# Layer 0's two feed-forwards as one, value projections of 512 columns, and 32 low parts made during block 1

## The chip, the cores and the metric

The kernel runs on one core of a Trainium2 chip. The metric is the device time of one execution in microseconds (us).

## The reference

Two residual blocks over 256 tokens of 1024 features. The first block runs once; the second has two layers over a token stream `x` and a context stream `ctx`. Cut to the parts that the change touches:

```python
def _ffn(h, p):
    return (jax.nn.silu(h @ p['w_ff_gate']) * (h @ p['w_ff_up'])) @ p['w_ff_down']

for l in range(DEPTH_2):                                  # 2 layers
    hc = _modulate(xc, mod_c[0], mod_c[1])
    if last:
        mem = _context_memory(hc, p)
    else:
        yc, mem = _context_mixer(hc, p)                   # attention, GLA, convolution, gates
        xc = _post(xc, yc, mod_c[2], ln1_g[l], ln1_b[l])
        xc = _post(xc, _ffn(_modulate(xc, mod_c[3], mod_c[4]), p), mod_c[5], ln2_g[l], ln2_b[l])
    x = _post(x, _latent_mixer(_modulate(x, sh1, sc1), mem, cos, sin, p), g1, ln1_g[l], ln1_b[l])
    x = _post(x, _ffn(_modulate(x, sh2, sc2), p), g2, ln2_g[l], ln2_b[l])
```

Both streams use the same weights in layer 0, the mixer's and the feed-forward's. Everything is float32.

## The kernel before

Activations lie with features on the partitions, 8 tiles of 128 features by 256 tokens. All weights are packed into "units" of 128 x 1024 float32 (512 KB), read one after another in the order in which the program asks for them (`unit`, L438). `unit` loads the raw unit four ahead (SP's DMA queue, 5 buffers) and splits it two ahead (`load`, L455): ScalarE writes the high part `whi` as float32r, GpSimd or VectorE writes the low part `wlo` = raw - high (`split`, L420; `lo_eng`, L373, deals them out by a ratio for each phase, `LO`: 1 of 2 on GpSimd in block 1 and layer 0's feed-forward, 1 of 3 in block 1's feed-forward, 3 of 5 in layer 0's mixers). `whi` and `wlo` have 3 buffers each. A product is three float32r products (`mm3`, L472): high x high, weight high x activation low, weight low x activation high; for a unit that is 24 matmuls of 256 columns. In layer 1 some parts multiply the raw float32 unit instead (`native`).

Layer 0's mixer runs twice with the same 109 units, for the context and then for the tokens. The first run stores each low part in DRAM (`kept`), the second reads it back in place of computing it. Projections that need tokens on the partitions (values) go through `tok` (L515): the activation is the stationary operand, the weight moves, 256 columns at a time; the names are `memv`, `foxv`, `sbv`, `v0`, `vg0`. In `mix` (L1449) a fixed interleaving steps attention, the units `glu0`, the gated-linear-attention levels (`gF`, `cum`, `am`) and, at low priority, the convolution `ca` on VectorE, 31 steps a tile; then come `gb0_0`, `r0`, `gb1_0`, `gb2_0` and `out0`.

After the two mixers layer 0's feed-forward runs for the context, then for the tokens: 44 gate/up units and 24 down units each (8 of them with 6 blocks in place of 8). While one stream's units run, the other stream's layer norms (`post`, `modulate`) run on VectorE and ScalarE, and 12 steps of the next layer's modulation matmuls (`ada`) are put in between. A scheduler orders each engine's instructions by the program's order and priorities; engines run their queues in order. Matmul results use three PSUM buffers (`mmp`).

The change touches `_plan`, `_pack`, `unit`/`load`, `block1`, `mem_kv`, `fox`, `stick`, `gla_in`, `gla_pair`, `gla_state`, `modulate`, `mix` and `program`.

## Time and profile before

| | |
|---|---|
| median of 3 runs | 3046.5 us (3044.25 to 3047.64) |
| profiled execution, its own time | 3039.65 us |
| its span, first to last instruction | 3037.4 us |
| mean granted TensorE clock | 0.971 |
| TensorE matmul / weight load busy | 2808.7 us (92%) / 2638.7 us (87%) |
| VectorE / ScalarE / GpSimd busy | 1965.5 us (65%) / 1412.3 us (46%) / 919.9 us (30%) |
| DMA | 578.33 MB, mean 190 GB/s |

PE is TensorE's matmul side, PEld its weight loads, DVE VectorE, ACT ScalarE, POOL GpSimd, SP the engine whose queue issues the transfers. Busy time of matmuls is pipelined: each record is longer than the distance to the next. The granted clock is the share of full speed at which TensorE was let run. Stages, by the first unit of each: block 1's mixers to 655 us, its feed-forward to 888, layer 0's context mixer to 1376, token mixer to 1804, feed-forwards to 2245 (the context's to 2027), layer 1's memory and mixer to 2788, its feed-forward to 3017, the last norm to the end.

### The profile page before, as it was taken

The page shows a single profiled execution, that of the slowest core. Times are in us where ns is not written, and L with a number is a line of the kernel's source. Part 1 is how long each engine was busy: PE and PEld are TensorE (multiplying, and loading weights), DVE is VectorE, ACT ScalarE, POOL GpSimd, SP SyncE. Part 2 cuts the span into 40 slices and gives each one's busy share as a digit, 9 for nine tenths or more (in the row PEclk, how much of TensorE's full clock was granted, in tenths as well). Part 3 has the DMA queues.
Part 4 walks back from the last instruction along what each step waited for, and adds up shares of the span by engine and source line. Part 5 has one row for each costly group of instructions (what it writes and reads, how often), then busy time and mean ns, then how long its engine had stood idle before and what let it go on. Part 6 is the DMA issues. An engine that isn't in the chain of part 4 may idle for free.

```text
span 3037.4 us, 52212 instructions
## 1 busy us (share of the span) xinstructions
PE 2808.7 (92%) x20992; PEld 2638.7 (87%) x20992; DVE 1965.5 (65%) x3305; ACT 1412.3 (46%) x2135; POOL 919.9 (30%) x684
## 2 busy tenths in 40 slices
PE   6999999999898878799999999999999999998898
PEld 6899988888898777788899988998888787898898
DVE  7586643447855999966897354367344599674554
ACT  5465556544445433445545554445334332354443
POOL 3253322333334445540102113444320113463000
PEclk9999999999999989899999999999999999999999
DMA  5444335566466554787666887655743223354353
GB/s 191 143 156 146 126 133 174 199 238 243 149 221 236 194 202 168 256 310 281 214 245 242 326 297 259 240 188 177 247 148 116 95 97 125 112 167 139 131 177 110
DMA packets 153426, 578.33 MB, mean 190 GB/s; under 512 B 17628, under 2 KB 17756, under 8 KB 146656
## 3 DMA queue, kind: packets, MB, share of 16 engines
q1 hardware_dynamic: 152496, 574.45, 54.9%
q8 instruction: 164, 2.69, 0.4%
q10 hardware_dynamic: 688, 0.56, 0.1%
q14 instruction: 78, 0.64, 0.1%
HBM read 516.73 MB, written 58.20 MB: 189 GB/s over the span
## 4 chain that ended last, share of the span: by engine, by line
PE 45%; DVE 19%; ACT 4%; DMA 2%; POOL 1%; issue 1%; SPq 0%; ACTq 0%; DVEq 0%; POOLq 0%
PE mm L371 38%; DVE ca L364 7%; DVE gF L361 2%; PE st L371 2%; DMA raw<-in_ws 2%; PE av L371 1%; POOL wlo L361 1%; DVE wlo L361 1%; PE ga L371 1%; ACT whi L358 1%; DVE sq L361 1%; PE ad L371 1%; DVE cum L1245 1%; DVE ht L364 1%; DVE fsum L584 1%
## 5 line engine op out<-in xcount | busy, mean ns | idle before, releaser
L358 ACT ACTIVATE whi<-raw 128x1024 fp32r<-128x1024 f32 (+1 forms) x706 | 736.1, 1046 | 819.5 <-PE mm L371 527.9
L361 POOL TENSOR_TENSOR wlo<-raw,whi 128x1024 fp32r<-128x1024 f32 (+1 forms) x282 | 713.6, 2532 | 1046.5 <-ACT whi L358 827.8
L361 DVE TENSOR_TENSOR wlo<-raw,whi 128x1024 fp32r<-128x1024 f32 (+1 forms) x315 | 399.6, 1269 | 384.7 <-ACT whi L358 375.0
L371 PE MATMUL mm<-hh,whi 128*128 128x256 f32 x3376 | 506.4, 292 | 17.8 <-ACT hh L358 5.5
L371 PE MATMUL mm<-hh,wlo 128*128 128x256 f32 x3376 | 494.0, 288 | 15.2 <-DVE wlo L361 10.2
L371 PE MATMUL mm<-hl,whi 128*128 128x256 f32 x3376 | 490.8, 287 | 0.0
L371 PEld LDWEIGHTS mm<-hh,whi 128*128 128x128 f32 x3376 | 450.0, 196 | 41.5 <-ACT hh L358 8.7
L371 PEld LDWEIGHTS mm<-hh,wlo 128*128 128x128 f32 x3376 | 446.7, 195 | 18.6 <-DVE wlo L361 10.6
L371 PEld LDWEIGHTS mm<-hl,whi 128*128 128x128 f32 x3376 | 445.9, 195 | 1.5 <-issue 1.0
L364 DVE SCALAR_TENSOR_TENSOR ca<-yp,pv,ca 128x256 f32<-128x256 f32 x720 | 360.6, 555 | 2.0
L371 PE MATMUL mm<-yh,whi 128*128 128x256 f32 x1152 | 174.2, 291 | 14.3 <-ACT yh L358 11.0
L371 PE MATMUL mm<-h,raw 128*128 128x256 f32 x800 | 181.9, 381 | 0.0
L361 POOL TENSOR_TENSOR gF<-cum 128x128 f32<-128x128 f32 x192 | 99.0, 547 | 256.8 <-PE ga L371 143.9
L371 PE MATMUL mm<-yh,wlo 128*128 128x256 f32 x1152 | 168.6, 289 | 5.3 <-DVE wlo L361 4.0
L371 PEld LDWEIGHTS mm<-yh,whi 128*128 128x128 f32 x1152 | 154.4, 195 | 20.7 <-ACT yh L358 14.2
L371 PE MATMUL mm<-yl,whi 128*128 128x256 f32 x1152 | 169.4, 289 | 1.3 <-DVE yl L364 1.3
L371 PEld LDWEIGHTS mm<-h,raw 128*128 128x128 f32 x800 | 150.3, 191 | 19.3
L371 PEld LDWEIGHTS mm<-yh,wlo 128*128 128x128 f32 x1152 | 154.0, 198 | 6.5 <-DVE wlo L361 4.2
L371 PEld LDWEIGHTS mm<-yl,whi 128*128 128x128 f32 x1152 | 154.0, 197 | 2.0 <-DVE yl L364 1.6
L371 PE MATMUL mm<-hidh,whi 128*128 128x256 f32 x704 | 102.4, 286 | 0.8 <-ACT hidh L358 0.8
L371 PE MATMUL mm<-hidl,whi 128*128 128x256 f32 x704 | 101.9, 285 | 0.0
L371 PE MATMUL mm<-hidh,wlo 128*128 128x256 f32 x704 | 101.0, 284 | 0.7 <-DVE wlo L361 0.7
(283 smaller groups left out, 3808.6 us busy)
## 6 DMA issues: line engine op xcount, KB each, us to landing
raw<-in_ws SPq DMA_DIRECT2D x744, 512.0 KB, 4.0
lo<-wlo SPq DMA_DIRECT2D x109, 512.0 KB, 3.3
wlo<-lo SPq DMA_DIRECT2D x109, 512.0 KB, 4.1
wada<-in_wa SPq DMA_DIRECT2D x48, 1024.0 KB, 7.0
raw<-in_ws SPq DMA_DIRECT2D x32, 384.0 KB, 3.1
memt<-in_tok SPq DMA_DIRECT2D x4, 256.0 KB, 4.9
xt<-in_tok SPq DMA_DIRECT2D x1, 1024.0 KB, 6.2
ct<-in_tok SPq DMA_DIRECT2D x1, 1024.0 KB
```

What stands on the lines that cost most here:

```text
L358: return self.nc.scalar.activation(out, in_, f, **k)
L361: return (eng or self.nc.vector).tensor_tensor(out=out, in0=a, in1=b, op=op)
L364: return self.nc.vector.scalar_tensor_tensor(out=out, in0=a, scalar=s, in1=b, op0=op0, op1=op1)
L371: return self.nc.tensor.matmul(out, lhsT=l, rhs=r, start=start, stop=stop, **k)
L584: self.nc.vector.tensor_reduce(out=s, in_=x.rearrange("p f n -> p n f"), axis=AX.X, op=ALU.add)
L1245: nc.vector.tensor_tensor_scan(out=o, data0=self.ones_t, data1=a, initial=0.0, op0=ALU.mult, op1=ALU.add)
```

## The change

- Layer 0's feed-forward (`both_ffn`) takes both streams at once: `joint_h` keeps their high (X) and low (Y) activations side by side, and a unit's matmuls move 512 columns. The first 6 feature tiles (`LEAD`) are done for the context alone and later again for the tokens; the last down chunk is done for the context, then for the tokens. Down sums are added to the streams chunk by chunk.
- The values `memv`, `foxv`, `sbv` and `vg0` are packed for `wide`: the weight moves 512 columns, two PSUM buffers collect the two token tiles, and four units make four feature tiles of values at once.
- `ahead` reads the 32 units of `glu0` and `gb0_0` during block 1, splits them and stores the low part; both runs of the mixer then read it.
- Activations and some mixer tiles share the two places X and Y of a new pool `hj`.

```diff
     def load(self, raw, n, i, _, native):
-        if native:
+        if native is True:
             return raw, None
         hi = self.wp.tile([P, 1024], F32R, tag="whi", name="whi", bufs=3)
         lo = self.wp.tile([P, 1024], F32R, tag="wlo", name="wlo", bufs=3)
-        kept = self.kept.pop(i, None)
+        if native == "ahead":
+
+            self.split(raw, hi, lo)
+            kept = self.kept[i] = self.dp.tile([P, 1024], F32, tag=f"lo{i}", name="lo")
+            self.nc.sync.dma_start(kept, lo.bitcast(F32))
+            return None
+        kept = self.kept.get(i)
...
+    def ahead(self):
+
+        for name in ("glu0", "gb0_0"):
+            for i in range(16):
+                self.unit(POS[name] + i, native="ahead")
+                yield
...
+    def wide(self, name, c, h):
+        ps = [self.mmp.tile([P, 512], F32, tag="mm", name="mm") for _ in range(2)]
+        for u in range(4):
+            hi, lo = self.unit(POS[name] + 4 * c + u)
+            for n, (x, part) in enumerate(((h[0], hi), (h[1], hi), (h[0], lo))):
+                for t in range(2):
+                    for k in range(2):
+                        self.mm(ps[t], x[:, 2 * u + k, t * P:(t + 1) * P], part[:, k * 512:(k + 1) * 512],
+                                start=u + n + k == 0, stop=u == 3 and n == 2 and k == 1)
+            if u == 1:
+                yield
+        yield ps
...
-            weave((stick, 3), (bf, 1), (take(fill, 8), 1))
+            self.pre = self.ahead()
+            weave((stick, 3), (bf, 1), (take(fill, 8), 1), (take(self.pre, 9), 1))
             run(bf)
-            weave((self.branch(2, h, ys, acc, False), 2), (take(fill, 4), 1))
+            weave((self.branch(2, h, ys, acc, False), 2), (take(fill, 4), 1), (take(self.pre, 4), 1))
...
+    def both_ffn(self, l, xs, adas, bp):
...
+        def hidden(ft, v=None):
...
+            if v is None:
+                pg, pu = [self.mmp.tile([P, 512], F32, tag="mm", name="mm") for _ in range(2)]
+                for j, ps in enumerate((pg, pu)):
+                    self.mm3(ps, self.unit(POS[f"gu{l}"] + 2 * ft + j), both, KT, 0)
+                s, c = self.t("cv", 512), slice(0, 2 * T)
+            else:
+                pg, pu = self.proj_pair(f"gu{l}", ft, self.h_of(v))
+                s, c = self.t("cv"), slice(v * T, (v + 1) * T)
+            self.act(s, pg, AF.Silu)
+            self.tt(s, s, pu, ALU.mult)
+            self.split(s, hid[ft][0][:, c], hid[ft][1][:, c])
...
+        for ft in range(self.LEAD):
+            hidden(ft, 1)
+            yield
+        self.act(xs[0], xs[0], scale=ALPHA)
+        for ft in range(self.LEAD, CHUNKS[0]):
+            hidden(ft)
+            yield
+        for ft in range(self.LEAD):
+            hidden(ft, 0)
+            yield
...
+            if c + 1 < len(CHUNKS):
+                for f in range(KT):
+                    down(c, k, f)
+                    yield
+            else:
+                for v in (1, 0):
+                    for f in range(0, KT, 2):
+                        down(c, k, f, v)
+                        yield
...
-        step(ffn, 10)
+        for _ in range(10):
+            step(ffn, 1)
+            step(b.pre, 1)
         run(fill0)
...
+        for _ in range(4):
+            step(ffn, 1)
+            step(b.pre, 2)
+        run(ffn, b.pre)
...
+            ffn = b.both_ffn(0, (xt, ct), (ax0, ac0), bp)
+            step(ffn, 1)
+            weave((b.modulate(xt, ax0, 3, got, lambda: b.h_of(0)), 2), (take(ffn, b.LEAD - 1), 1))
+            for i in range(16):
                 step(ffn, 2)
-                for i in range(9):
-                    step(g, 2)
+                step(fill1, 1)
+            step(ffn, 10)
+            f32 = b.place("X")
+            g = chain(b.post(ct, "l2g0", "l2b0"),
+                      b.modulate(ct, ac1, 0, got, lambda: (f32[:, 0], Nones()), native=True))
+            for i in range(KT):
+                step(g, 2)
+                if i % 2:
                     step(ffn, 1)
-                run(g)
...
```

The new order on GpSimd in the context mixer, among the levels of gated linear attention (`gF`); `wlo` are low parts, `yp` edges of convolution tiles. Before:

```order
L361 TENSOR_TENSOR gF<-cum 128x128 x4
L361 TENSOR_TENSOR wlo<-raw,whi 128x1024 x2
L361 TENSOR_TENSOR gF<-cum 128x2x64 x4
L361 TENSOR_TENSOR gF<-cum 128x4x32 x4
L361 TENSOR_TENSOR wlo<-raw,whi 128x1024 x2
L361 TENSOR_TENSOR gF<-cum 128x8x16 x4
L361 TENSOR_TENSOR wlo<-raw,whi 128x1024
L361 TENSOR_TENSOR gF<-cum 128x16x8 x4
L361 TENSOR_TENSOR wlo<-raw,whi 128x1024 x2
L361 TENSOR_TENSOR gF<-cum 128x32x4 x4
L361 TENSOR_TENSOR wlo<-raw,whi 128x1024
```

and now:

```order
L366 TENSOR_TENSOR gF<-cum 128x128 x4
L366 TENSOR_TENSOR wlo<-raw,whi 128x1024
L366 TENSOR_TENSOR gF<-cum 128x2x64 x4
L366 TENSOR_TENSOR gF<-cum 128x4x32 x4
L366 TENSOR_TENSOR wlo<-raw,whi 128x1024 x2
L366 TENSOR_TENSOR gF<-cum 128x8x16 x4
L366 TENSOR_TENSOR gF<-cum 128x16x8 x4
L1509 MEMSET yp 128x15
L1510 MEMSET yp 128x15
L366 TENSOR_TENSOR gF<-cum 128x32x4 x4
```

Here 8 low parts have become 3; over the whole context mixer GpSimd has 48 in place of 67 and VectorE 13 fewer.

TensorE at the start of layer 0's feed-forward, context units (`hh`/`hl` before, `hX`/`hY` now are the activations' high and low parts); `st<-fsum` and `st<-sq` are the sums of the token stream's norms. Before, the post-norm's sum of squares is the last one in this part:

```order
L371 MATMUL mm<-hh,whi 128x256 x8
L371 MATMUL mm<-hl,whi 128x256 x7
L371 MATMUL st<-sq,ones 128x256
L371 MATMUL mm<-hl,whi 128x256
L371 MATMUL mm<-hh,wlo 128x256 x8
```

and now both sums of the modulate follow, and 24 modulation matmuls, ahead of the lead's ninth unit:

```order
L376 MATMUL mm<-hX,wlo 128x256 x8
L376 MATMUL st<-fsum,ones 128x256
L376 MATMUL mm<-hX,whi 128x256 x8
L376 MATMUL mm<-hY,whi 128x256 x8
L376 MATMUL mm<-hX,wlo 128x256 x8
L376 MATMUL mm<-hX,whi 128x256 x8
L376 MATMUL mm<-hY,whi 128x256 x8
L376 MATMUL mm<-hX,wlo 128x256 x8
L376 MATMUL st<-sq,ones 128x256
L376 MATMUL ad<-wada,sc 32x256 x24
L376 MATMUL mm<-hX,whi 128x256 x8
```

Four units later the first matmuls of 512 columns stand.

TensorE at the end of that stage (`hidh`, `hidl`: hidden features; `raw` with `h` or `hX`: layer 1's first unit). Before:

```order
L371 MATMUL mm<-hidh,whi 128x256 x6
L371 MATMUL mm<-hidl,whi 128x256 x6
L371 MATMUL mm<-hidh,wlo 128x256 x6
L1159 MATMUL ad<-cc,adas 128x128 x2
L371 MATMUL mm<-h,raw 128x256 x8
```

and now the context's modulate has its sums in the last down unit and behind it:

```order
L376 MATMUL mm<-hidh,whi 128x256 x5
L376 MATMUL st<-fsum,ones 128x256
L376 MATMUL mm<-hidh,whi 128x256
L376 MATMUL mm<-hidl,whi 128x256 x6
L376 MATMUL mm<-hidh,wlo 128x256 x6
L376 MATMUL ad<-wada,sc 32x256 x8
L376 MATMUL st<-sq,ones 128x256
L1208 MATMUL ad<-cc,adas 128x128 x2
L376 MATMUL mm<-hX,raw 128x256 x7
```

All the waits of layer 1's first unit on the context's norms, which stood among the token stream's units before, now stand in the last 8 short units and behind them.

## Rows read from the trace of the kernel before

**Rows 1.** Stages: us; busy PE, PEld, DVE, ACT, POOL; PEclk, DMA share, GB/s.
```profile
479.00:888.00 409.00, 393.74 (x3230) 362.96 (x3229) 240.56 (x311) 199.88 (x298) 131.54 (x80) 0.98 0.58 199
888.00:1376.00 488.00, 412.90 (x3018) 396.17 (x3016) 403.01 (x659) 214.61 (x312) 234.29 (x181) 0.92 0.66 231
1376.00:1804.00 428.00, 407.77 (x3091) 391.36 (x3092) 294.29 (x660) 229.16 (x332) 55.72 (x89) 0.99 0.76 272
1804.00:2245.00 441.00, 425.40 (x3584) 403.10 (x3583) 218.81 (x255) 191.20 (x277) 181.38 (x107) 0.98 0.62 216
```

**Rows 2.** TensorE timeline, first units of layer 0's feed-forward: start, us, instruction, count, idle before.
```profile
1804.37 1.12 PE L371 MATMUL mm<-hh,whi 128*128 128x256 f32 x8
1805.33 1.12 PE L371 MATMUL mm<-hl,whi 128*128 128x256 f32 x8
...
1809.35 0.70 PE L371 MATMUL st<-fsum,ones 128*128 128x256 f32 x2 [1.35 <-DVE fsum L584]
...
1818.95 0.67 PE L371 MATMUL st<-sq,ones 128*128 128x256 f32 x2 [1.97 <-DVE sq L361]
...
1831.76 2.08 PE L371 MATMUL mm<-hh,whi 128*128 128x256 f32 x8 [3.82 <-DVE cv L361]
```

**Rows 3.** TensorE timeline: one-column matmuls, then float32 of 512 and of 256 columns.
```profile
89.33 1.05 PE L371 MATMUL st<-ones,hsq 128*128 128x1 f32 x8
90.25 0.48 PE L371 MATMUL mm<-hh,whi 128*128 128x256 f32 x2
...
2276.82 7.07 PE L371 MATMUL mm<-h,raw 128*128 128x256 f32 x32
2283.72 0.81 PE L371 MATMUL mm<-raw,h 128*128 128x256 f32 x3
...
2324.20 1.02 PE L371 MATMUL st<-hsq,ones 128*128 128x512 f32 x2
2325.06 1.24 PE L371 MATMUL mm<-raw,h 128*128 128x256 f32 x5
```

**Rows 4.** Busy time from `glu0` to the end of `gb0_0`: context mixer, token mixer.
```profile
954.80:1195.70 240.90, 196.47 (x1377) 187.46 (x1376) 227.52 (x406) 100.95 (x144) 114.56 (x102) 0.90 0.55 191
1459.70:1655.40 195.70, 189.89 (x1411) 181.90 (x1410) 186.61 (x448) 98.27 (x136) 31.84 (x58) 0.98 0.65 231
```

**Rows 5.** Convolution steps, context then token mixer: ns min/median/max; then busy time of both.
```profile
L364 DVE SCALAR_TENSOR_TENSOR ca<-yp,pv,ca x225: 458/473/2673, 987.4 to 1247.5; 128x256 f32<-128x256 f32 x113
...
L364 DVE SCALAR_TENSOR_TENSOR ca<-yp,pv,ca x240: 462/482/619, 1470.0 to 1657.2; 128x256 f32<-128x256 f32 x120
...
988.00:1250.00 262.00, 145.21 (x232) 0.00 (x0) 0.89 0.55 192
```

**Rows 6.** Context mixer, instructions on `wlo` alone: us; PE, PEld, DVE, POOL busy; PEclk.
```profile
988.00:1250.00 262.00, 65.34 (x399) 57.49 (x400) 23.27 (x19) 93.46 (x31) 0.89 0.55 192
```

**Rows 7.** VectorE timeline at layer 1's start: post-norm and modulate of the token stream.
```profile
2245.18 0.87 DVE L364 SCALAR_TENSOR_TENSOR xt<-mm,ada,xt 128x256 f32<-128x256 f32 x2 [6.69 <-PE mm L371]
...
2265.30 3.65 DVE L584 TENSOR_REDUCE fsum<-xt 128x256 f32<-128x2048 f32 x1 [0.66 <-ACT xt L358]
...
2280.57 1.28 DVE L364 SCALAR_TENSOR_TENSOR ht<-xc,ada,nr 128x256 f32<-128x256 f32 x3
...
2289.05 0.46 DVE L364 SCALAR_TENSOR_TENSOR hl<-ht,ada,hh 128x256 fp32r<-128x256 f32 x1
```

**Rows 8.** The page: high parts, low parts, and the stores of low parts (KB, us to landing).
```profile
L358 ACT ACTIVATE whi<-raw 128x1024 fp32r<-128x1024 f32 (+1 forms) x706 | 736.1, 1046 | 819.5 <-PE mm L371 527.9
L361 POOL TENSOR_TENSOR wlo<-raw,whi 128x1024 fp32r<-128x1024 f32 (+1 forms) x282 | 713.6, 2532 | 1046.5 <-ACT whi L358 827.8
...
L361 DVE TENSOR_TENSOR wlo<-raw,whi 128x1024 fp32r<-128x1024 f32 (+1 forms) x315 | 399.6, 1269 | 384.7 <-ACT whi L358 375.0
...
lo<-wlo SPq DMA_DIRECT2D x109, 512.0 KB, 3.3
```

**Rows 9.** Busy time of the 20 us in which DMA moved most.
```profile
1328.00:1348.00 20.00, 17.94 (x135) 16.49 (x134) 11.77 (x11) 9.09 (x16) 9.57 (x4) 1.00 0.95 346
```

More of the change, by code (lines that the diff above doesn't have):

```diff
@@ L945, in proj_v @@
         def proj_v(f):
-            v = bp.tile([P, 2, T], F32, tag="av", name="fv", bufs=2)
-            self.act(v, self.tok("foxv", f // 2, h))
+            v = self.values("foxv", f, h, bp)
             return v
@@ L1005, in fox_turn, with values @@
         return p
+    def values(self, name, f, h, bp):
+        if f % 4 == 0:
+            self.vs = [bp.tile([P, 2, T], F32, tag="av", name="v", bufs=2) for _ in range(2)]
+            for t, ps in enumerate(self.wide_now(name, f // 4, h)):
+                for i, v in enumerate(self.vs):
+                    self.act(v[:, t], ps[:, i * T:(i + 1) * T])
+        return self.vs[f // 2 % 2]
     def softplus_abs(self, out, z):
@@ L1186, in rope, with gla_in @@
         self.tt(t, t, sw, ALU.add)
-    def gla_in(self, l, h, bp, with_q):
+    def gla_in(self, l, h, bp, with_q, room=None):
         nc = self.nc
-        qk = bp.tile([P, 4, 2, T], F32, tag="C", name="qk")
+        qk = bp.tile([P, 4, 2, T], F32, tag="C", name="qk") if room is None else \
+            room[:, 1].rearrange("p (a b) n -> p a b n", b=2)
         glr = bp.tile([P, T], F32, tag="glr", name="glr")
@@ L1210, in pair @@
                 yield
-            vg[hp] = bp.tile([P, 2, 512], F32, tag="vg", name="vg", bufs=2)
+            vg[hp] = (bp.tile([P, 4, T], F32, tag="vg", name="vg", bufs=2) if room is None else
+                      room[:, 0, 4 * hp:4 * hp + 4]).rearrange("p (a b) n -> p a b n", b=2)
+            if l == 0:
+                for got in self.wide(f"vg{l}", hp, h):
+                    for t, ps in enumerate(got or ()):
+                        self.act(vg[hp][:, t], v3(ps))
+                    yield
+                return
             for i in range(2):
-                self.act(vg[hp][:, :, i * T:(i + 1) * T], self.tok(f"vg{l}", f + i, h))
+                self.act(vg[hp][:, :, i], self.tok(f"vg{l}", f + i, h))
                 yield
@@ L1373, in modulate @@
         yield
-        h = self.new_h(pool, native)
+        h = new()
         hh, hl = h[:2]
@@ L1447, in glu, with mix @@
             yield
-    def mix(self, l, h, x, ada, mem, bp, keep, then=None):
+    def mix(self, l, h, x, ada, mem, bp, keep, then=None, room=None):
         nc = self.nc
         self.act(x, x, scale=ALPHA)
-        qk, vg, glr, gates, pairs = self.gla_in(l, h, bp, True)
+        qk, vg, glr, gates, pairs = self.gla_in(l, h, bp, True, room)
         S = mem[2] if mem else None
@@ L1484, in mix @@
         run(att, side, gla[0])
-        acc = bp.tile([P, 4, T], F32, tag="vg", name="acc", bufs=2)
+        acc = bp.tile([P, 4, T], F32, tag="vg", name="acc", bufs=2) if room is None else room[:, 0]
         acc = [acc[:, f] for f in range(4)]
@@ L1664, in program @@
+        with b.pool("m1") as bp, b.phase("m1t", t1=4, t2=6, t4=4):
+            run(b.post(xt, "l2g0", "l2b0"))
+            h = b.modulated(xt, ax1, 0, lambda: b.new_h("Y") + (f32[:, 1],), native="both")
+            b.native = True
+            mem = b.ctx_memory(1, got[3], bp, rp)
+            b.native = False
+            b.some_f32 = True
+            b.mix(1, h, xt, ax1, mem, bp, bp)
         with b.pool("f1") as bp, b.phase("f1t", t1=10, t2=6):
-            h = b.modulated(xt, ax1, 3, fast=True)
+            h = b.modulated(xt, ax1, 3, lambda: b.new_h("Y"), fast=True)
```

135 lines of the change are left out of this document (80 added, 55 removed).

## The prediction

> **What bounds the kernel now.** Read first the busy time by stage [rows 1]: each stage's own width against its engines. TensorE is near full everywhere but in one: layer 0's context mixer (888 to 1376 us) takes 488 us with a granted clock of 0.92, the token mixer behind it, which runs the same code, 428 us at 0.99. Since matmul records overlap, their busy time says little about pace, so read next the distance from start to start [rows 2]: a row of 8 float32r matmuls of 256 columns begins 0.96 us after the one ahead of it, so 0.120 us a matmul, and a weight unit (24 matmuls) costs 2.88 us.
>
> What sets the 0.120 is in [rows 3]. A plain float32 matmul instruction takes 6.90/32 = 0.216 us at 256 columns and 0.86/2 = 0.43 us at 512: twice the columns, twice the time, so this stream is set by columns, and half of 0.216 (float32 here runs each column twice as long) is 0.108. Eight matmuls of one column take 0.92, 0.115 each: what a weight load leaves as the least distance. 0.120 is nearer to the load than to the columns, so a float32r matmul of 256 columns waits for its weights.
>
> Third, the two mixers in the stretch from the first unit of `glu0` to the last of `gb0_0` [rows 4]: 240.9 us (context) and 195.7 us (tokens), VectorE busy 94% and 95%. VectorE is the bound there. The convolution step shows why its work is dearer in the first [rows 5]: median 473 ns against 482, but a longest of 2673 against 619. A step that meets one of GpSimd's low-part subtractions waits for its end. In 988 to 1250 us GpSimd makes 31 of them (93 us) and VectorE 19 (23 us) [rows 6].
>
> **Joint feed-forward, matmuls.** Removed: 48 of 136 weight units of layer 0's two feed-forwards (32 gate/up, 16 down), each with a load, a high part on ScalarE and a low part. In their place 48 units run 24 matmuls of 512 columns instead of 2 x 24 of 256: 1152 pairs of 0.240 us become matmuls of 0.43/2 = 0.215. Bounds: 0.240 (nothing gained) and 0.215; I take 0.216, from the float32 row of the same width, because the load of 0.115 is then far below the columns. 1152 x 0.024 = **-27.6 us**.
>
> The Trainium skill ("TensorE: Matmul & The Clock Gate", Back-to-back issue gap) gives 131 ns for a sustained stream of weight load and matmul at 512 columns and 216 for an isolated one. By the first the term would be 1152 x 0.109 = -126 us (an estimate); the rows have no 512-column stream under 0.215 a pass, so they speak for the second.
>
> **Joint feed-forward, its two ends.** Before, each chain (post-norm, then modulate) ran under a whole feed-forward of the other stream. Undisturbed, at layer 1's start [rows 7], the post-norm takes 2265.30 - 2245.18 = 20.1 us, the first modulated tile follows after 15.3 more, all of it 44.
>
> *Start.* The token chain now has only the lead as cover: six feature tiles of the context, 12 x 2.88 = 34.6 us. In the new order the modulate's two sums stand ahead of units 7 and 9. The first is ready at 20.1 + 3.7 (reduction) plus the low parts between, about 29 us; TensorE is there at 6 x 2.88 plus the two waits that exist already (1.35 and 1.97 [rows 2]) and half-clock matmuls, about 23: 6 idle. The second comes some 8 us later: 2.4 idle. Unit 9 then needs a PSUM buffer that VectorE frees only behind the reciprocal root, 4 more idle, as the 3.82 us wait for `cv` did before. About 15 against 7.1 now: **+8**.
>
> *End.* The context's chain starts when its last down units end; as cover stand the token stream's 8 short down units (2.16 us each, 17.3) and 8 steps of the modulation matmuls (6.9): 24 us. Layer 1's first unit needs the first modulated tile, at 35.4 us and with 5 low parts and 8 residual adds on VectorE about 42: **+16** idle (at least 35.4 - 24 = 11).
>
> *Rest.* 253 (88 gate/up units) + 127 (down) + 21 (modulation matmuls) + 3 (sums) = 404 us of matmuls stand against 441 measured [rows 1]: 37 idle, 30 without the start. With half the splits, half the weight traffic in the joint part and no second chain under a full-speed stream I take 16 of it: **-14**; bounds 0 and -25.
>
> So the stage: -27.6 + 8 + 16 - 14, about **-18 us**.
>
> **Wide values.** 40 unit runs (memory, fox and stick values 8 each, `vg0` twice 8) have 12 matmuls of 512 columns in place of 24: 480 x 0.024 = 11.5 us at most. The context mixer's 96 are under VectorE, the memory values' 96 in the waiting start; 288 x 0.024 = 6.9 count. `wide` holds two of the three PSUM buffers, about 1 us: **-6**. Moving the copies to ScalarE (the same columns, other shapes) lies beside TensorE: nothing; uncovered it is under 1 us a call.
>
> **Low parts made ahead.** In the context mixer the 32 units of `glu0` and `gb0_0` now take their low part from DRAM, as the token mixer's do in the same place without a stall that shows [rows 4]. The new order has 19 fewer low parts on GpSimd there and 13 fewer on VectorE. Direct: 13 x 1.27 = 16.5 us of VectorE [rows 8]. Indirect: the 225 convolution steps between 988 and 1250 [rows 5] would cost 225 x 0.473 = 106 at their median, and 145 less 3 for seven first steps, 142, are measured: 36 us of waiting for 31 subtractions, so 19 fewer return about 22; other instructions a few more: 42 in all. VectorE was 94% busy, so the stretch shortens by that: **-42 us**. Bounds: 16.5 (only the direct part), 60 (all of the difference between the mixers, 488 - 428).
>
> In block 1 the same 32 splits are added: 13 in the stick branch and the two gates, 10 in the last 20 gate/up units, 9 in the down projection. No matmul, but ScalarE 1.05 and GpSimd 2.53 or VectorE 1.27 each [rows 8], a 512 KB load and a 512 KB store on SP's queue. The engines have room (there VectorE is busy 241 of 409 us, ScalarE 200, GpSimd 132 [rows 1]). Two things don't: over 20 gate/up units (57.6 us) 20 loads plus 10 loads and stores are 21 MB, 364 GB/s, and the densest slice seen moved 346 [rows 9]: 3 us. And high and low parts have 3 buffers: where two ahead units follow each other (the down projection), the next real unit's split starts only when TensorE has finished the one before, about 2 us, four times: 8. Store waits on SP hold loads that are asked for four units early: nothing, else 3 us each. **+12**; bounds 0 and 32 x 3.6 = 115.
>
> **Sum.** -18 - 6 - 42 + 12 = -54 us against the profiled execution's 3039.65: 2985.7. The runs' median, 3046.5, lies 6.9 above that execution; the forecast for the median is **2992.5 us**.
>
> **The rivals.**
> 1. *VectorE's relief is only the direct part* (the mixer then waits on its attention and state chains): 25 us less gain, 3018. For it: waits for `gw`, `pr` and `am` sit in that stretch too. Against: the token mixer has them as well and needs 196 us there.
> 2. *512 columns cost 0.240*: 27.6 + 6.9 back, 3027. Against it stand the one-column and 512-column rows.
> 3. *The splits ahead are exposed*, the slower side: an ahead unit keeps one of three high/low buffers until its store has landed (3.3 us [rows 8] behind 1.05 + 2.53), and the next real unit waits. All of it exposed is 115 us, 103 above my term: 3095. From 2.0 us per ahead unit on (65 us) the change is slower than before. For it: the buffers are not increased. Against: ahead units stand mostly alone, with a real unit's 2.88 us on either side.
> 4. *A 512-column matmul keeps the distance of a 256-column one*, 0.120: 1440 x 0.096 = 138 more, 2855. The 131 ns of the Trainium skill ("TensorE: Matmul & The Clock Gate", Back-to-back issue gap) would be of this kind. Against: [rows 3] doubles.
> 5. *Both chains cost twice*: 24 more, 3017.
> 6. *Two of the gains fail together* (1 and 2): 25 + 34.5, 3052: no change.
> That the change doesn't do what it says is excluded by the order: 512-column matmuls and the missing subtractions stand in it.
>
> **How the numbers follow.** Forecast 0.64 (its own range 2965 to 3015: the mixer between 25 and 55, block 1 between 0 and 25, the ends 10 either way); rival 1 0.12, rival 2 0.08, rival 3 0.07, rival 4 0.02, rival 5 0.02, rival 6 0.05. Faster by over 0.2% (about what a measurement of this kernel can tell from no change): 0.64 + 0.12 + 0.08 + 0.02 + 0.02 = 0.88; same 0.05 (rival 6); slower 0.07 (rival 3). The range 2950 to 3032 takes in rivals 1, 2 and 5 and leaves out 3, 4, 6 (0.14) and the edges of the forecast.
>
> **What would show it.** Right: joint matmuls 0.216 apart; layer 0's feed-forward stage about 424 us with two idle groups on TensorE, near its start (waits on `fsum`, `sq`, `cv`) and before the first `hX,raw`; the stretch `glu0` to `gb0_0` of the context mixer near 199 us, with no convolution step queue behind GpSimd. Wrong: 0.240 there; that stretch over 220; block 1 (first instruction to the first unit of layer 0) longer by over 25 us.

## The result, and the profile after

| | before | after |
|---|---|---|
| median of the runs | 3045.4 us | 3006.4 us (3003.7 to 3011.5) |
| ratio, 95% interval | | 0.9884 [0.986, 0.9908] |
| profiled execution: its time, span | 3039.65, 3037.4 us | 3003.74, 3001.9 us |

The change makes the kernel 1.2% faster. The forecast was 2992.5 us with a range of 2950 to 3032: right direction, the time inside the range, the gain smaller by a quarter to a third (39 us by the medians, 35.5 by the spans, 54 said). One of the ten executions of e5_gp_dummy took 4983.3 us at a mean granted clock of 0.82; its median and range below are of the other nine. The page of the changed kernel (the part on engines, and the splitting into high and low parts):

```profile
span 3001.9 us, 48842 instructions
PE 2772.0 (92%) x19360; PEld 2536.1 (84%) x19360; DVE 1877.7 (63%) x3298; ACT 1391.0 (46%) x2095; POOL 810.6 (27%) x643
...
L363 ACT ACTIVATE whi<-raw 128x1024 fp32r<-128x1024 f32 (+1 forms) x690 | 718.4, 1046 | 819.2 <-PE mm L376 476.0
L366 POOL TENSOR_TENSOR wlo<-raw,whi 128x1024 fp32r<-128x1024 f32 (+1 forms) x232 | 579.9, 2502 | 966.7 <-ACT whi L363 654.9
L366 DVE TENSOR_TENSOR wlo<-raw,whi 128x1024 fp32r<-128x1024 f32 (+1 forms) x317 | 413.4, 1305 | 441.6 <-ACT whi L363 335.9
```

GpSimd makes 50 low parts fewer and VectorE 2 more: 48 fewer in all, one for each unit that the joint feed-forward no longer loads a second time. ScalarE makes 16 high parts fewer (48 gone, 32 made ahead). Busy time by stage in the changed kernel, columns and stages as [rows 1], by the first unit of each (start to block 1's feed-forward, that feed-forward, context mixer, token mixer, joint feed-forward, layer 1's memory and mixer), and last the stretch from `glu0` to `gb0_0` in the context mixer [rows 4]:

```profile
0.00:671.90 671.90, 614.10 (x4573) 557.13 (x4573) 392.55 (x679) 380.96 (x615) 238.35 (x134) 0.99 0.55 186
671.90:917.00 245.10, 217.98 (x1761) 206.48 (x1760) 161.71 (x203) 117.61 (x171) 72.23 (x56) 0.94 0.72 245
917.00:1357.60 440.60, 399.46 (x2914) 378.11 (x2914) 351.00 (x648) 214.69 (x313) 178.26 (x162) 0.97 0.75 263
1357.60:1784.10 426.50, 405.95 (x2999) 385.19 (x3000) 294.09 (x660) 227.83 (x330) 57.58 (x88) 0.99 0.76 272
1784.10:2211.90 427.80, 403.91 (x2427) 337.32 (x2426) 177.66 (x236) 137.53 (x191) 118.75 (x75) 0.98 0.47 164
2211.90:2786.20 574.30, 530.05 (x3075) 473.56 (x3075) 390.31 (x735) 220.21 (x348) 143.56 (x126) 0.98 0.36 119
...
988.30:1187.10 198.80, 184.77 (x1330) 173.67 (x1329) 191.23 (x428) 101.38 (x144) 65.85 (x85) 0.97 0.67 234
```

Set beside the trace of before, cut at the same units:

| stage | before, us | after, us | difference |
|---|---|---|---|
| start to the first gate/up unit of block 1 | 662.2 | 671.9 | +9.7 |
| block 1's feed-forward | 226.5 | 245.1 | +18.6 |
| layer 0, context mixer | 487.4 | 440.6 | -46.8 |
| layer 0, token mixer | 428.3 | 426.5 | -1.8 |
| layer 0, feed-forwards | 440.8 | 427.8 | -13.0 |
| layer 1 up to its feed-forward | 576.3 | 574.3 | -2.0 |
| the rest | 215.9 | 215.7 | -0.2 |

The sum is -35.5. The context mixer gave more than forecast (42), and the stretch of [rows 4] came down from 240.9 to 198.8 us (199 was said). Block 1 took back 28.3 us, and the joint feed-forward gave 13 in place of 18.

Now the joint stage from the inside. The timeline of TensorE at its start (start, us, instruction, count, idle before):

```profile
1789.06 0.70 PE L376 MATMUL st<-fsum,ones 128*128 128x256 f32 x2 [1.37 <-DVE fsum L620]
...
1798.85 0.67 PE L376 MATMUL st<-sq,ones 128*128 128x256 f32 x2 [2.13 <-DVE sq L366]
...
1813.15 1.22 PE L376 MATMUL st<-fsum,ones 128*128 128x256 f32 x2 [6.81 <-DVE fsum L620]
...
1823.12 0.67 PE L376 MATMUL st<-sq,ones 128*128 128x256 f32 x2 [1.27 <-DVE sq L366]
...
1829.02 1.21 PE L376 MATMUL mm<-hX,whi 128*128 128x256 f32 x8 [2.49 <-DVE cv L366]
...
1855.16 1.98 PE L376 MATMUL mm<-hX,wlo 128*128 128x512 f32 x8
1856.97 1.98 PE L376 MATMUL mm<-hX,whi 128*128 128x512 f32 x8
```

Five waits, 14.1 us, where [rows 2] had 7.1: 7.0 more, where 8 was forecast. The last two rows are joint matmuls of 512 columns: eight of them begin 1.81 us after the eight ahead; over nine such groups (1842.47 to 1858.79) that is 0.2266 us each, not 0.216. At the end of the stage, with the last matmuls of the context's down units first:

```profile
2170.76 0.88 PE L376 MATMUL mm<-hidh,wlo 128*128 128x256 f32 x6
...
2176.47 0.70 PE L376 MATMUL st<-fsum,ones 128*128 128x256 f32 x2 [0.77 <-DVE fsum L620]
...
2199.26 0.70 PE L376 MATMUL st<-fsum,ones 128*128 128x256 f32 x2 [2.04 <-DVE fsum L620]
...
2206.57 0.67 PE L376 MATMUL st<-sq,ones 128*128 128x256 f32 x2 [2.52 <-DVE sq L366]
...
2211.91 1.65 PE L376 MATMUL mm<-hX,raw 128*128 128x256 f32 x3 [4.45 <-ACT hX L363]
```

These four waits (9.8 us) are for the context's norms, which have only the token stream's short down units and the modulation steps as cover; 16 had been said.

### The profile page after: what moved, and what is told of

It reads as the page before. It is cut to its first block, busy times and chain, and to the rows that moved or that the text cites. A ratio compares the mean times of both kernels' runs of the same rounds, so it can differ in the third digit from the quotient of the medians.

```text
span 3001.9 us, 48842 instructions
## 1 busy us (share of the span) xinstructions
PE 2772.0 (92%) x19360; PEld 2536.1 (84%) x19360; DVE 1877.7 (63%) x3298; ACT 1391.0 (46%) x2095; POOL 810.6 (27%) x643
## 5 line engine op out<-in xcount | busy, mean ns | idle before, releaser
L376 PE MATMUL mm<-hY,whi 128*128 128x256 f32 (+1 forms) x3312 | 482.0, 297 | 22.1 <-ACT whi L363 12.0
L376 PEld LDWEIGHTS mm<-hY,whi 128*128 128x128 f32 x3312 | 438.6, 195 | 43.4 <-ACT whi L363 14.0
L376 PE MATMUL mm<-hX,whi 128*128 128x256 f32 (+1 forms) x1520 | 242.7, 308 | 7.0 <-DVE gt L369 3.4
L376 PEld LDWEIGHTS mm<-hX,whi 128*128 128x128 f32 x1520 | 212.4, 195 | 20.5 <-DVE gt L369 3.6
L376 PE MATMUL mm<-hY,wlo 128*128 128x256 f32 x1432 | 205.6, 285 | 1.0 <-POOL wlo L366 1.0
L376 PE MATMUL mm<-hX,raw 128*128 128x256 f32 x800 | 185.0, 385 | 4.4 <-ACT hX L363 4.4
L376 PEld LDWEIGHTS mm<-hY,wlo 128*128 128x128 f32 x1432 | 187.1, 193 | 1.4 <-POOL wlo L366 1.2
L376 PE MATMUL mm<-hX,wlo 128*128 128x256 f32 (+1 forms) x984 | 169.5, 314 | 10.6 <-DVE wlo L366 8.3
L376 PEld LDWEIGHTS mm<-hX,raw 128*128 128x128 f32 x800 | 152.1, 193 | 24.5 <-ACT hX L363 4.7
L376 PEld LDWEIGHTS mm<-hX,wlo 128*128 128x128 f32 x984 | 143.7, 193 | 21.9 <-DVE wlo L366 8.7
L376 PE MATMUL mm<-hidh,wlo 128*128 128x256 f32 (+1 forms) x576 | 99.7, 314 | 11.4 <-DVE wlo L366 9.2
```

The costliest lines, as they stand in the source:

```text
L376: return self.nc.tensor.matmul(out, lhsT=l, rhs=r, start=start, stop=stop, **k)
```

## The experiments

Each kernel is the changed one with one edit. Medians of the kernel before, taken again beside these kernels, lay between 3042.2 and 3046.4 us, so the stages of the traces count for more than the totals. The token mixer alone lasted 426.5 to 434.7 us in profiled executions of kernels that leave it untouched.

### e1_no_ahead: the change without the low parts made ahead

```diff
     def ahead(self):
-        for name in ("glu0", "gb0_0"):
+        for name in ():
```

> The changed kernel without the low parts made ahead; the joint feed-forward and the wide values stay. Theory A (the two traces): the context mixer, which went from 487 to 441 us with the change, goes back to about 487 (+47), and block 1, whose end moved from 888.7 to 917.0 us, gives back what the ahead units cost there, about 32 us: the sum is +12 to +18 us, 3019 to 3024. Theory B (the prediction's terms, 42 gained and 12 paid): +30 us, 3036. Theory C (block 1 is longer because of the wide values or the moved buffers, not of the ahead units): block 1 keeps its end near 917 us and the whole is +47, 3053.

3022.7 us (3019.2 to 3030.4), ratio to before 0.9926 [0.9908, 0.9945]: theory A. Busy time of the stick branch, the gate/up units, the down projection and the context mixer in this run:

```profile
402.10:572.50 170.40, 165.81 (x1229) 143.97 (x1227) 62.10 (x99) 106.49 (x157) 48.44 (x20) 1.00 0.48 167
660.20:811.80 151.60, 147.12 (x1228) 135.44 (x1228) 112.63 (x132) 64.38 (x108) 52.72 (x41) 0.97 0.55 202
811.80:887.00 75.20, 66.84 (x537) 65.80 (x536) 50.81 (x62) 34.15 (x45) 16.94 (x9) 0.98 0.50 173
887.00:1370.40 483.40, 414.48 (x2916) 392.04 (x2915) 401.75 (x659) 213.96 (x312) 229.85 (x181) 0.92 0.65 233
```

Against the changed kernel (180.7, 155.5, 89.6 and 440.6 us) the ahead units cost 10.3 us beside the stick branch, 3.9 among the gate/up units and 14.4 in the down projection; block 1 ends at 887.0 in place of 917.0, so they cost 30.0 us in all. They give 42.8 in the mixer. The forecast for that gain was 42, for the cost 12.

What the stick branch pays is seen in TensorE's waits in it. In the changed kernel (total, times, longest):

```profile
PE z L376 <- DVE se L366: 9.9, 7, 2.2
```

and without the ahead units:

```profile
PE z L376 <- DVE se L366: 3.8, 3, 1.3
```

6.1 of the 10.3 us are waits for `se`, a sum on VectorE. In the down projection of the changed kernel TensorE's waits are 16.8 us in all, where this run has 8.4; one alone is 9.2 us. The stage, then TensorE in it:

```profile
827.40:917.00 89.60, 71.63 (x536) 70.49 (x534) 53.00 (x61) 40.14 (x51) 26.76 (x12) 0.89 0.67 229
...
852.52 1.12 PE L376 MATMUL mm<-hidh,whi 128*128 128x256 f32 x8
853.48 1.12 PE L376 MATMUL mm<-hidl,whi 128*128 128x256 f32 x8
863.82 2.08 PE L376 MATMUL mm<-hidh,wlo 128*128 128x256 f32 x8 [9.22 <-DVE wlo L366]
```

and VectorE at that time:

```profile
854.13 1.67 DVE L369 SCALAR_TENSOR_TENSOR ht<-xc,ada,nr 128x256 f32<-128x256 f32 x4
855.73 2.54 DVE L369 SCALAR_TENSOR_TENSOR hX<-ht,ada,hX 128x256 fp32r<-128x256 f32 x1
...
861.37 1.26 DVE L369 SCALAR_TENSOR_TENSOR hX<-ht,ada,hX 128x256 fp32r<-128x256 f32 x3
862.56 2.08 DVE L366 TENSOR_TENSOR wlo<-raw,whi 128x1024 fp32r<-128x1024 f32 x2
```

TensorE had used this unit's high part from 852.52 on. Its low part was made only from 862.56 on, behind the whole chain of the context's modulate (`ht`, `hX`) on VectorE. One step of that chain lasts 2.54 us, some 2 us more than the others of its kind, and GpSimd makes a low part at the same time:

```profile
855.38 2.62 POOL L366 TENSOR_TENSOR wlo<-raw,whi 128x1024 fp32r<-128x1024 f32 x1 [5.21 <-ACT whi L363]
```

The wait has a second price: the granted clock of the stage is 0.89, against 0.98 in this run, and the eight matmuls behind the wait take 1.87 us until the next eight begin (863.82 to 865.69), where the eight ahead of it took 0.96. Two units are split ahead, and the ahead units count among them; the next run asks whether that is why the split came too late.

### e8_own_bufs: the ahead units of the feed-forward in buffers of their own

```diff
-        while self.n_ready < min(len(self.asked) + self.AHEAD, len(self.order)):
+        m, real = len(self.asked), 0
+        while m < min(len(self.asked) + 4, len(self.order)) and real < self.AHEAD:
+            real += self.order[m][2] != "ahead" or self.ap is None
+            m += 1
+        while self.n_ready < m:
...
+                hi, lo = self.ap.tile([P, 1024], F32R, tag="ahi", name="whi", bufs=1), raw.bitcast(F32R)
...
-    self.phase("b1ft", t1=10, t2=6)
+    self.phase("b1ft", t1=8, t2=5)
```

> The changed kernel with the ahead units of block 1's feed-forward in a high-part buffer of their own (the low part is written over the raw unit), and the count of two units that are split ahead counts real units alone there; 3 of 16 temporaries are given up for the room. Theory A (an ahead unit takes the place of a real one among the two that are split ahead): the stalls of 9.2, 4.0 and 2.2 us in the down projection go for the most part, the projection from 89.6 to 78 to 82 us, the gate/up units from 155.5 to 153: -8 to -13 us, 2993 to 2998. Theory B (the cost is the ahead units' own time on VectorE and GpSimd ahead of a real one's): 0 to -3 us. Theory C (fewer temporaries slow the feed-forward): slower than 3006.

3005.7 us (3004.9 to 3008.9). Where the edit is, theory A nearly holds: the down projection lasts 82.8 us in place of 89.6 (78 to 82 said) and the 9.2 us wait is gone; gate/up 154.6 in place of 155.5. The edit frees the look-ahead and the buffers at once, so the two together are about half of the 14.4 us, and which of them it is, is not shown. Waits of 4.8 us for high parts, which the changed kernel does not have there, come in. The total is no better, and misses A: the mixers lasted 442.3 and 433.8 us in this execution, 1.7 and 7.3 more than in the changed kernel. Whether that is connected or the mixers' own scatter is open.

### e3_ahead_early: other places for the ahead units

```diff
+            self.pre = self.ahead()
...
             for i in range(12):
                 step(fox, 1)
+                step(self.pre, 1)
...
-        for _ in range(10):
-            step(b.pre, 1)
+        for i in range(10):
+            step(b.pre, i < 7)
```

> The changed kernel with the 32 ahead units at other places: 12 in the fox branch, 9 with the stick branch, 4 in the third gate, 7 among the gate/up units, none in the down projection of block 1. Theory A: what an ahead unit costs depends on its place, and the stalls of 9.2, 4.0 and 2.2 us in the down projection come from real units that are split too late behind the norms' chain on VectorE: the down projection goes from 89.6 back to about 77 us, the gate/up units lose some 3, the fox branch pays 3 to 5: -8 to -14 us, 2992 to 2998. Theory B (each ahead unit costs about 1 us of TensorE's time wherever it stands): 0, 3003 to 3010. Theory C (they hurt more among the fox branch's chains): slower by 5 or more.

2997.8 us (2996.8 to 3001.7): theory A, 8.7 us faster than the change. Block 1 ends at 906.1 in place of 917.0. The down projection lasts 78.8 us, the gate/up units 149.3; the fox branch pays 9.2 for its 12 units (169.6 to 178.8 us), where A had said 3 to 5.

### e5_gp_dummy: GpSimd's work put back, without its results

```diff
             if kept is not None:
+                if ... and i not in self.seen:
+                    self.seen.append(i)
+                    if len(self.seen) * 3 // 5 != (len(self.seen) - 1) * 3 // 5:
+                        self.tt(self.dum, raw, raw, ALU.subtract, self.nc.gpsimd)
                 self.nc.sync.dma_start(lo.bitcast(F32)[:, :n], kept[:, :n])
```

> The changed kernel with 19 GpSimd subtractions of 128x1024 put back into the context mixer, at the units glu0 and gb0_0, on data that nothing uses; the low parts still come from DRAM and VectorE's 13 subtractions stay away. Theory A (a convolution step that meets a GpSimd subtraction waits for its end): the longest convolution step goes back from the change's value to about 2.6 us and the context mixer from 441 to 463 to 469 us: 3028 to 3034 in all. Theory B (GpSimd's subtractions cost VectorE nothing, the gain came from VectorE's 13 and from TensorE not waiting for low parts): 0 to +5 us, 3006 to 3011.

3035.9 us (3031.3 to 3047.0), ratio to before 0.9979 [0.9963, 0.9994]: three quarters of the change's gain are gone. The context mixer as a whole:

```profile
915.60:1383.90 468.30, 405.85 (x2914) 384.10 (x2914) 377.86 (x648) 214.98 (x313) 220.97 (x181) 0.94 0.71 248
```

27.7 us longer than in the changed kernel, with VectorE's busy time 26.9 us higher for the same 648 instructions. 19 operations that nobody waits for, on another engine, cost VectorE 1.4 us apiece (26.9 / 19). Little of it falls on the convolution: VectorE's instructions on `ca` take 143.8 us in place of 137.0, those on `gF` 52.3 in place of 40.2. The added operations also hold the raw unit a little longer, which can delay a load but not lengthen an instruction of VectorE. Theory A holds in size; the sign named for it was a poor one, since the changed kernel already has a convolution step of 2621 ns: its GpSimd still makes 48 low parts there.

### e9_lo_vector: no low parts on GpSimd in layer 0's mixers

```diff
-LO = {..., "m0t": (3, 5), ...}
+LO = {..., "m0t": (0, 1), ...}
```

> The changed kernel with all low parts of layer 0's mixers on VectorE, where 3 of 5 were on GpSimd: 48 subtractions move in the context mixer, 12 of them into the stretch from glu0 to gb0_0. Theory A (run e5_gp_dummy: 19 GpSimd subtractions cost that stretch 27.7 us, 1.46 each, more than the 1.27 us of one on VectorE): the move is worth 0 to 4 us there, and outside it VectorE has room: the context mixer 436 to 442 us, 3002 to 3008 in all. Theory B (the work counts where it runs): 48 x 1.27 = 61 us more for VectorE, of which 12 to 20 show: 3018 to 3026.

2975.4 us (2969.5 to 2981.4), ratio to before 0.977 [0.975, 0.979]: both theories miss it, 31 us faster than the change. The context mixer:

```profile
915.20:1327.30 412.10, 391.94 (x2914) 373.39 (x2915) 351.56 (x705) 216.77 (x316) 46.77 (x107) 0.98 0.80 284
```

28.5 us shorter. VectorE has 57 instructions more, 47 of them subtractions of some 1.2 us (most of the others are low parts of activations), and its busy time is the same (351.6 against 351.0). So GpSimd's subtractions had cost VectorE as much as making them itself does, and not in the VectorE-bound stretch alone, where theory A had looked for it: from `glu0` to `gb0_0` the run takes 188.1 us (982.4 to 1170.5) against 198.8, which is 10.7 of the 28.5. With the busy time the same, the 28.5 us must come from when things are ready. TensorE's waits in the stage fall from 39.9 to 20.8 us, and its busy time by 7.5 (399.5 to 391.9). The largest part of the waits is for low parts (total, times, longest), in the changed kernel

```profile
PE mm L376 <- DVE wlo L366: 9.1, 3, 5.8
...
PE mm L376 <- POOL wlo L366: 2.8, 3, 1.3
```

and in this run

```profile
PE mm L376 <- DVE wlo L366: 0.3, 1, 0.3
```

The other waits fall by some 7.5 us, for results of VectorE, of ScalarE and for transfers. How GpSimd's work reaches TensorE is seen at `r0` in the changed kernel. VectorE:

```profile
1193.15 15.07 DVE L369 SCALAR_TENSOR_TENSOR ca<-yp,pv,ca 128x256 f32<-128x256 f32 x15
1208.14 1.21 DVE L366 TENSOR_TENSOR wlo<-raw,whi 128x1024 fp32r<-128x1024 f32 x1
```

15 convolution steps last 15.07 us, and the low part behind them begins at 1208.14. GpSimd meanwhile makes two low parts and, between and behind them, other operations of two inputs (`sr`, `yl`), to 1207.9:

```profile
1197.27 2.41 POOL L366 TENSOR_TENSOR wlo<-raw,whi 128x1024 fp32r<-128x1024 f32 x1
1199.65 1.80 POOL L366 TENSOR_TENSOR sr<-sr,hY 128x256 f32<-128x256 f32 x2
...
1202.93 2.41 POOL L366 TENSOR_TENSOR wlo<-raw,whi 128x1024 fp32r<-128x1024 f32 x1
```

and TensorE, at the end of it:

```profile
1209.41 2.08 PE L376 MATMUL mm<-hX,wlo 128*128 128x256 f32 x8 [5.82 <-DVE wlo L366]
```

The same place in this run, VectorE:

```profile
1173.83 1.22 DVE L366 TENSOR_TENSOR wlo<-raw,whi 128x1024 fp32r<-128x1024 f32 x1
1174.97 2.06 DVE L369 SCALAR_TENSOR_TENSOR ca<-yp,pv,ca 128x256 f32<-128x256 f32 x5
```

Five steps take 2.06 us, and no low part stands behind more than five. The 8 units of `r0` last 23.0 us here (8 x 2.88), 31.5 in the changed kernel.

### e2_split_cols and e4_pace: what 512 columns are worth

```diff
-                    self.mm3(ps, self.unit(POS[f"gu{l}"] + 2 * ft + j), both, KT, 0)
+                    w = self.unit(POS[f"gu{l}"] + 2 * ft + j)
+                    for q in range(2):
+                        self.mm3(ps[:, q * T:(q + 1) * T], w, streams[q], KT, 0)
```

> The changed kernel with every joint matmul of 512 columns made as two of 256 with the same weight block; loads, splits and order of the units stay. Theory A: the trace's paces, 0.2266 us at 512 columns against 0.120 at 256, differ by 0.0134 us a pair, 1152 pairs: +15 us, 3022, nearly all of it in the 48 joint units. Theory B (the prediction's 0.024 a pair): +27 us, 3034. Theory C (the joint stage is held by its low parts or its loads, not by TensorE's pace): 0 to +5 us.

3027.2 us (3016.6 to 3033.8). By the totals it lies between A and B; by the stage it is A: from the first joint-stage unit to layer 1's first the run takes 445.0 us against 427.8, 17.2 more. 14.9 of them lie between the first unit for both streams and the short down units (312.7 us in the changed kernel, 327.5 here), where TensorE has no wait over 0.3 us in either; A's sum is 15.4.

```diff
+            for x, todo in ((h[0], (64, 128, 256, 384, 512)), (xt, (64, 128, 256, 384, 512))):
+                for n in todo:
+                    ...
+                    for i in range(64):
+                        b.mm(ps[:, :n], x[:, i % 8, :P], flatx[:, i % 4 * 512:i % 4 * 512 + n], ...)
```

> The changed kernel with ten series of 64 matmuls behind layer 1's feed-forward, whose results are not used: float32r, then float32, each with 64, 128, 256, 384 and 512 columns, a new weight block for each. Theory A (a matmul costs its columns and a constant): float32r 0.067 us at 128, 0.120 at 256, 0.173 at 384, 0.227 at 512. Theory B (the prediction: up to 256 columns the weight load of 0.115 sets the distance): 0.115 to 0.120 at 64, 128 and 256, then the columns. Float32: 0.43 at 512 and 0.216 at 256 under both; at 64 and 128 columns 0.05 to 0.11 by A, 0.115 by B.

One execution, 3221.1 us with the added series. TensorE's timeline in windows inside the series (first start, us to the last end, count): float32r of 64, 128, 256, 384 and 512 columns, then float32 of 512, where each matmul is recorded as two passes:

```profile
2986.01 3.96 PE L376 MATMUL mm<-hY 128*128 128x64 f32 x34
2995.65 12.57 PE L376 MATMUL mm<-hY 128*128 128x128 f32 x58
3014.83 3.88 PE L376 MATMUL mm<-hY 128*128 128x256 f32 x31
3019.20 10.56 PE L376 MATMUL mm<-hY 128*128 128x384 f32 x60
3030.82 12.43 PE L376 MATMUL mm<-hY 128*128 128x512 f32 x54
3142.59 52.95 PE L376 MATMUL mm<-xt 128*128 128x512 f32 x123
```

With the last matmul's own length taken off (0.2 to 0.6 us), float32r takes from start to start 0.112 us at 64 columns, 0.120 at 256, 0.1735 at 384, 0.227 at 512 (for 512: (12.43 - 0.39) / 53), all at a granted clock of 1.00; float32 of 512 takes 0.429 a pass. Neither theory has it whole. There is a floor of 0.112, as B said. But 256 columns already lie above it: each further 128 columns add 0.053, and what is left at zero columns is 0.013 (0.227 - 4 x 0.0535). A float32 pass runs each column twice as long and has almost none of that constant: 0.429 is 2 x 0.2146, and four times 0.0535 is 0.214. For 128 columns there is no distance at full clock: that series ran at a granted clock of 0.50, 0.213 us from start to start.

### e6_end_cover and e7_lead8: cover for the two chains

```diff
                 for v in (1, 0):
+                    for ft in todo:
+                        hidden(ft, v)
+                        yield
                     for f in range(0, KT, 2):
```

> The changed kernel with the last four feature tiles of the joint feed-forward made for the context, then its last down sums, then the four tiles again for the tokens and theirs: 8 more unit loads, and 23 us more of TensorE's work as cover for the context's norms. Theory A: the waits before layer 1's first unit (0.8, 2.0, 2.5 and 4.5 us in the changed kernel's trace) and the half clock behind them go; against them 96 matmuls of 512 columns become 192 of 256, +2.6 us of loads: -6 to -10 us, 2996 to 3000. Theory B (the context's chain is late for another reason, VectorE's own load): the waits stay, +3 us.

3001.8 us (2997.7 to 3004.5). The wait of 4.5 us before layer 1's first unit is gone, and the part from the last gate/up units to that unit takes 99.7 us against 102.1: 2.4 us, less than A said. The joint stage as a whole stays (427.1 against 427.8).

```diff
-    LEAD = 6
+    LEAD = 8
...
-            step(ffn, 1)
+            step(ffn, 2)
```

> The changed kernel with a lead of 8 feature tiles in place of 6, and the tokens' modulate begun one tile later: its sums stand one tile later on TensorE. Theory A: of the 14.1 us of waits at the start of the joint stage (1.4, 2.1, 6.8, 1.3, 2.5) 6 to 9 go, and the two more tiles cost 1.3 us: -4 to -8 us, 2998 to 3002. Theory B (the chain moves back with the tile that starts it, so the same waits come later): 0 to +2 us.

3007.7 us (3003.0 to 3021.0): theory B, no gain. The waits at the start are still 1.4, 2.0, 3.9, 0.9 and 2.5 us; the 6.8 became 3.9 in front of another tile. The waits are 3.5 us less in all, but the stage lasts 428.5 us, against 427.8.

### e11_wide_split: what the wide values are worth

```diff
-                        self.mm(ps[t], x[...], part[:, k * 512:(k + 1) * 512], ...)
+                        for q in range(2):
+                            self.mm(ps[t][:, q * T:(q + 1) * T], x[...], part[:, k * 512 + q * T:k * 512 + (q + 1) * T], ...)
```

> The changed kernel with each 512-column matmul of the wide value projections made as two of 256: 480 more matmuls, the same units, buffers and copies. Theory A (0.0134 us a pair, 288 of the 480 not hidden): +4 us, 3010; at most 6.4. Theory B (all of it lies under other waits): 0 to +1. Theory C (the prediction's 0.024 a pair): +7 to +11.

3010.4 us (3007.9 to 3012.1), 4 us above the change's median: what A said, though the two ranges overlap, so the 4 us are not clear of the scatter.

### e10_combo and e12_best: putting gains together

e10_combo is e3_ahead_early with 6 ahead units beside the stick branch and 7 in the third gate, and with e6_end_cover's edit.

> The changed kernel with the ahead units at other places (12 in the fox branch, 6 with the stick branch, 7 in the third gate, 7 among the gate/up units, none in the down projection) and the last four feature tiles made for each stream apart. Theory A (the gains of e3_ahead_early and e6_end_cover add up, and 3 units moved from the stick branch, at 1.1 us each, to the gate, at 0.2, give 2 to 3): 2990 to 2995. Theory B (what is saved is given back to later waits, as part of e8_own_bufs was): 2996 to 3002. Theory C (the third gate has no room for 7 loads and stores beside its own): slower than 3002.

3001.0 us (2996.4 to 3008.0): no better than either part. From the third gate to the end of block 1's output projection it takes 83.2 us where e3_ahead_early takes 76.3, so the 3 units more there cost 2.3 us each, not 0.2, and the stick branch gives back only 1.0 for its 3. What an ahead unit costs is not a price per unit that can be carried from place to place.

e12_best is e3_ahead_early with the low parts of both layers' mixers on VectorE (`"m0t": (0, 1)`, `"m1t": (0, 1)`).

> The places of e3_ahead_early (none in the down projection) together with the mixers' low parts on VectorE in both layers. Theory A (a GpSimd subtraction holds up a busy VectorE by at least its own price there; the two gains lie in different stages and add up): 2975.4 less 8.7 of e3_ahead_early and 0 to 5 in layer 1's mixer, 2961 to 2967. Theory B (part of what is saved is given back later, as in e10_combo): 2967 to 2975. Theory C (layer 1's mixer needs GpSimd's share, its units are not kept in DRAM): slower than 2975.

2947.6 us (2944.5 to 2950.9), ratio to before 0.969 [0.9673, 0.9707]: faster than both kernels, and 13 us below the range of theory A. Its context mixer, then layer 1 up to its feed-forward:

```profile
908.30:1317.50 409.20, 391.69 (x2917) 373.77 (x2916) 347.31 (x703) 215.60 (x315) 50.75 (x107) 0.97 0.78 280
2172.00:2730.60 558.60, 525.00 (x3074) 469.68 (x3074) 399.54 (x779) 220.61 (x348) 49.61 (x82) 0.99 0.35 122
```

Against the changed kernel: block 1 -8.7, context mixer -31.4, layer 1 -15.7 (558.6 against 574.3), which A had put at 0 to 5. No convolution step in it lasts longer than 959 ns, where the changed kernel's longest is 2621. Two things were not run: the mixers' low parts on VectorE without any ahead units, so whether those still pay then is open; and block 1's low parts on VectorE alone.

## Why the prediction was right, and where it was wrong

The range of 2950 to 3032 us was wide enough for three of the rivals, so a time inside it shows little by itself. Two terms missed by much, the 512-column matmuls by 12 us and block 1 by 18, both to the slower side; the end of the joint stage and the mixer gave back 7 to 11.

| term | forecast | measured | from |
|---|---|---|---|
| 512-column matmuls, joint stage | -27.6 | -15.4 | 1152 x (0.240 - 0.2266); e2: 14.9 to 17.2 |
| start of the joint stage | +8 | +7.0 | 14.1 - 7.1 us of waits |
| its end | +16 | +9.8 | four waits |
| rest of that stage | -14 | -14.4 | -13.0 less the three above |
| wide values | -6 | about -4 | e11 |
| context mixer | -42 | -42.8 to -46.8 | e1; the two traces |
| low parts made in block 1 | +12 | +30 | e1 |

The rows come from different runs and do not add up to the 35.5 us exactly. The rest of the joint stage is what the other rows leave, and no measurement of its own; 8.6 us of it can be seen: from 1835 us to the end of the stage the kernel before waited that long (for `sq`, `fsum` and `wlo`), and the changed kernel did not wait from 1835 us to the last down units.

**The mixer** was right in cause, and in size as a whole. VectorE was the bound, and the waits behind GpSimd were the larger part: 27.7 us of the stage return with 19 subtractions on GpSimd alone (e5), and 15.1 of the measured 42.8 are left for the direct part, where 13 x 1.27 = 16.5 was said. Inside VectorE the sum came out otherwise. Against e1 its busy time is 50.8 us lower (401.8 to 351.0): 23.5 on `ca`, where 22 was said for the convolution steps, 9.0 on low parts, where 16.5 was said (11 fewer in the stage, but the 30 that stay take 1.42 us each, not 1.26), and so about 18 on other instructions, for which I had "a few more". Rival 1, which allowed for the direct part only, is refuted. The Trainium skill ("SBUF — State Buffer", Who interferes with whom) states it as a rule: a VectorE instruction with two inputs in SBUF and a GpSimd instruction that reads SBUF exclude each other, and the second waits for the whole of the first. This case's traces agree: 26.9 us in e5, and an unchanged busy time with 57 instructions more in e9.

**The 512-column term** was mis-sized by a wrong neighbour. I took 0.216 us "from the float32 row of the same width". Float32r carries 0.013 us a matmul that float32 does not, so a pair gains 0.0134 us and not 0.024. My reading that a 256-column matmul "waits for its weights" was wrong as well: the least distance with a new weight block each time is 0.112 (64 columns), and 0.120 is columns plus that constant. A row of the same instruction and type, even at another width, would have been the better neighbour. Of the Trainium skill's two figures ("TensorE: Matmul & The Clock Gate", Back-to-back issue gap), 131 ns for a sustained stream and 216 isolated, the measured 227 ns stands beside the second. Rival 4, which rested on a price of the first kind, is refuted; so is rival 2 (0.240).

**Block 1** is the step that failed: I priced 3 us for DMA, 8 for the buffers in the down projection, and nothing for the 13 units beside the stick branch and the third gate, because "ahead units stand mostly alone, with a real unit's 2.88 us on either side" and "the engines have room". The stick branch cost 10.3, the gate/up units 3.9, the down projection 14.4, about half of which goes with the look-ahead and the buffers (e8). Average room on VectorE said nothing about a chain (`se` there, the modulate in the down projection) that TensorE waits for at that moment. Rival 3 is right in its place and a quarter of its size: 30 of 115 us, 0.9 us an ahead unit, below the 2.0 at which the change would have lost by the forecast's other terms.

**The ends** were roughly right. At the start 7.0 us came where 8 was said, in other pieces: 6.8, 1.3 and 2.5 us for 6, 2.4 and 4. At the end the first modulated tile reached TensorE 40.3 us behind the context's last down unit (2171.6 to 2211.9), near my 42. The cover was what I had too small: 40.3 less 9.8 of waits is 30.5 us, not 24. The 16 of the forecast was not even the difference of its own two numbers, 42 and 24, which is 18. Rival 5 (both chains twice as dear) is refuted, and so is rival 6, which needed 1 and 2.

Of the three signs named for being wrong, two did not come: the joint matmuls are not at 0.240, and the stretch from `glu0` to `gb0_0` is under 220. The third, block 1 longer by over 25 us, came with 28.3. Of the signs for being right, "no convolution step queue behind GpSimd" came only in part: 7 steps of the context mixer last over 1.5 us, where 21 did.

## What to carry to other kernels

Work dealt out to GpSimd beside a busy VectorE is not free: here each 128x1024 subtraction on GpSimd cost VectorE about what VectorE needed to make it itself, so count both engines as one before dealing work between them, and look for a group whose longest instance is several times its median. Work moved to an earlier stage "with room" is charged at the moment where it stands: look for the chain that runs there and for look-ahead counters and buffers that it shares with the work on the path. For the price of a wider instruction take a row of the same operation and type, and put the constant per instruction apart from the columns.

## What the runs showed of the hardware that was not expected

- With a new weight block for each, a float32r matmul of 256 to 512 columns takes its columns (0.053 us for 128 at a granted clock of 1.00) and 0.013 us; 64 columns take 0.112 from start to start; a float32 pass has almost no such constant (0.429 at 512 columns, twice the columns' 0.214).
- In the series of 64-column float32r matmuls the granted clock fell from 1.00 to 0.50 (2.4 to 1.2 GHz) while TensorE was busy without a gap; the distance went from 0.112 to 0.213 us. It stayed there through the whole series of 128 columns, at the same 0.213 us, and the first 23 matmuls of 256 columns took 0.213 too, before it rose again inside their series. Whether the kernel's own short matmuls ever do this is open.
- 19 GpSimd subtractions of which no result is used lengthened VectorE's busy time by 26.9 us and the context mixer by 27.7.
